# Sample attention's value products: two key heads in one stationary operand, new tokens of all sequences in two products of 512 columns

## The chip, the cores and the metric

The kernel runs on one core of a Trainium2 chip. The metric is the device time of one execution in microseconds (us). The engines are named as in the profile: PE is TensorE's matmul (PEld its weight loads), DVE VectorE, ACT ScalarE, POOL GpSimd, SP the queue of SyncE that issues most DMAs. Names such as L943 are lines of the kernel before; from L945 of it on, the changed kernel has the same code two lines earlier.

## The reference

One inference step of a hybrid decoder layer, all in float32: a prompt of 512 tokens and a sample batch of 8 sequences with 4 new tokens each pass through an input projection of 18,952 columns, an mLSTM branch (4 heads of 512), an attention branch (32 heads of 64, 4 key heads, a window of 128), and a gated merge with two projections, an output projection and a layer norm. The change lies in the attention of the sample batch:

```python
def _swa_sample(q, k_new, v_new, k_buf, v_buf, slopes, sinks):
    k_all = jnp.concatenate([k_buf, k_new], axis=1)
    v_all = jnp.concatenate([v_buf, v_new], axis=1)   # 128 kept rows and 4 new ones per sequence
    ...
    out = _sink_attend(q, k_all, v_all, dist, valid, slopes, sinks)

def _sink_attend(q, k, v, dist, valid, slopes, sinks):
    s = jnp.einsum('...qhgd,...khd->...hgqk', q, k) * (A_HEAD_DIM ** -0.5)
    ...
    p = jax.nn.softmax(jnp.concatenate([s, sink], axis=-1), axis=-1)[..., :-1]
    return jnp.einsum('...hgqk,...khd->...qhgd', p, v)
```

The last einsum is what the change computes in another way: per sequence and key head, 64 value columns, and 8 query heads times 4 tokens = 32 rows of probabilities over 128 kept and 4 new positions.

## The kernel before

The activations of all 544 tokens lie transposed in SBUF, and the columns of the input projection are worked through in pairs of 128 (function paired). A pair takes seven steps, the seven products of a Strassen-like scheme on half matrices; each step (half_product) multiplies one 128x1024 weight tile, split into a high and a low part, with 272 columns: 16 products on L634 and 8 on L636. The weights are loaded by SP (L205, L605) into a few buffers, summed by DVE (L614), cast to the high part by ACT (L212) and subtracted for the low part by DVE (L213). The results of a step are gathered on ACT, DVE and POOL (L644 to L663).

Beside this stream run Python generators: the prompt's attention, then the sample batch's (sample_attention), then the mLSTM state of the samples (samples). After each step a tick resumes every generator until its next yield; what it then emits stands in PE's program behind that step. PE's order is this order, written by hand; the other engines' order is chosen by a scheduler that goes by its own estimate of times.

In sample_attention the probabilities of the kept positions lie in E (128 rows = 32 heads x 4 tokens, per sequence 128 columns), those of the new positions in En (per sequence 32 columns, zero outside the own 4). The kept values are vb (128 positions, per sequence 4 key heads x 64), the new values of all sequences vas (32 rows). For each pair of sequences PE turns E and En (L929, L930), ACT and DVE copy the turned tiles out of PSUM (L934, L935), and two ticks later PE multiplies, per sequence and key head, vb's 64 columns with 32 columns of the turned E (L943) and adds vas's 64 columns times 32 columns of the turned En (L944). The 64 result rows of a key head go to the lower or the upper half of one PSUM tile by the tile position. So four groups of four transposes and four groups of 16 products stand between projection steps. At the end DVE multiplies the results into the gates gas (L950), SP stores them (L951), the pools t1 and t2 are closed, and the pools of the state are opened: its tiles C are loaded on SP (L990), the samples' q, k and v too (L1016), POOL makes four copies of k and v (L1000), and PE starts with L1028. Small PSUM tiles (sm) have four banks.

Of the kernel before, what the change touches and what calls it, by code (L numbers as in the profile page):

```python
# [15 lines left out]
F32 = mybir.dt.float32  # L16
# [6 lines left out]
NB = 8  # L23
# [8 lines left out]
KVH = 4  # L32
GRP = 8
# [47 lines left out]
def _build(tc, nc, i, o, es):  # L81
# [3 lines left out]
    def pool(stack, name, bufs, space=None, side=None):  # L85
        kw = {"space": space} if space is not None else {}
        if space is None:
            kw["side"] = side or "right"
            kw["reuse_waits"] = "tile"
        return stack.enter_context(tc.tile_pool(name=name, bufs=bufs, **kw))  # L90

    y_p, y_s, C_p, n_p, m_p, kb_p, vb_p, C_s, n_s, m_s, kb_s, vb_s = o
    V, A, G, PE = nc.vector, nc.scalar, nc.gpsimd, nc.tensor
# [29 lines left out]
    def nm(s):  # L123
        count[0] += 1
        return f"{s}_{count[0]}"

    def sm():
        return psB.tile([128, 512], F32, tag="sm", name=nm("sm"))
# [10 lines left out]
    def blk(ap, n=4):  # L139
        return ap.rearrange("p (b x) -> p b x", b=n)  # L140
# [21 lines left out]
    ident = cc[:, C_ID:C_ID + 128]  # L162
# [146 lines left out]
    for g in range(4):  # L309
# [9 lines left out]
        for q in range(4):  # L319
            pt = sm()  # L320
# [524 lines left out]
    esT = ExitStack()  # L845

    def sample_attention():
        t1, t2 = pool(esT, "t1", 1), pool(esT, "t2", 1)
        gas = t1.tile([128, 16, NS], F32, name="gas")
        qraw = t1.tile([128, 2, GRP, NS], F32, name="qraw")  # L850
        qas = t1.tile([128, 2, NB, GRP, NTS], F32, name="qas")
        kas = t1.tile([128, 2, NS], F32, name="kas")
        vas = t1.tile([32, 256], F32, name="vas")
        nc.sync.dma_start(gas[:], d_bra[:, :, SEQ:T].rearrange("k p t -> p k t"))
        nc.sync.dma_start(kas[:], d_ka[:, :, SEQ:T].rearrange("k p t -> p k t"))
        nc.sync.dma_start(vas[:], d_vr[SEQ:T])
        for kvh in range(KVH):
            half = slice((kvh % 2) * 64, (kvh % 2) * 64 + 64)
            for a in range(2):
                nc.sync.dma_start(qraw[half, kvh // 2, a::2],  # L860
                                  d_qa[kvh * 4:kvh * 4 + 4, a * 64:a * 64 + 64].rearrange("k p t -> p k t"))
        kb = t1.tile([128, NB, 256], F32, name="kb")
        vb = t1.tile([128, NB, 256], F32, name="vb")
        nc.sync.dma_start(kb[:], i["state_attn_k"].rearrange("b t k d -> t b (k d)"))
        nc.sync.dma_start(vb[:], i["state_attn_v"].rearrange("b t k d -> t b (k d)"))
        E = t1.tile([128, NB, 132], F32, name="E")
        En = t1.tile([128, NB, NS], F32, name="En")
        G.memset(En[:], 0.0)
        st = t1.tile([128, 4, NB], F32, name="sast")
        for _ in range(5):  # L870
            yield
        for j in range(2):
            V.tensor_scalar(qas[:, j], qraw[:, j].rearrange("p g (b t) -> p b g t", t=NTS), 0.125, None, op0=ALU.mult)

        def keysT(b2_):
            kTs = []
            for bb in range(2):
                pk = sm()
                for kk in range(2):
                    PE.transpose(pk[:, kk * 128:kk * 128 + 128], kb[:, b2_ * 2 + bb, kk * 128:kk * 128 + 128], ident)  # L880
                kT = t1.tile([128, 2, 128], F32, tag=f"kT{bb}", name=nm("kT"))
                A.copy(kT[:].rearrange("p a b -> p (a b)"), pk[:, 0:256])
                kTs.append(kT)
            return kTs

        kTs = keysT(0)
        for b2_ in range(4):
            yield
            ps_, pn_ = sm(), sm()
            for bb in range(2):  # L890
                b = b2_ * 2 + bb
                for kvh in range(KVH):
                    r = slice((kvh % 2) * 64, (kvh % 2) * 64 + 64)
                    q = qas[r, kvh // 2, b].rearrange("p g t -> p (g t)")
                    orow = slice(kvh * 32, kvh * 32 + 32)
                    tp = ((kvh % 2) * 64, kvh * 32)
                    PE.matmul(ps_[orow, bb * 128:bb * 128 + 128], q, kTs[bb][r, kvh // 2], start=True, stop=True, tile_position=tp)
                    PE.matmul(pn_[orow, bb * 4:bb * 4 + 4], q, kas[r, kvh // 2, b * 4:b * 4 + 4], start=True, stop=True, tile_position=tp)
            sl = slice(b2_ * 2, b2_ * 2 + 2)
            V.tensor_tensor(out=E[:, sl, 0:128], in0=blk(ps_[:, 0:256], 2),  # L900
                            in1=cc[:, C_SB:C_SB + 128].unsqueeze(1).to_broadcast([128, 2, 128]), op=ALU.add)
            V.tensor_tensor(out=E[:, sl, 128:132], in0=blk(pn_[:, 0:8], 2),
                            in1=cc[:, C_SB + 128:C_SB + 132].unsqueeze(1).to_broadcast([128, 2, 4]), op=ALU.add)
            if b2_ < 3:
                kTs = keysT(b2_ + 1)
        V.tensor_reduce(st[:, 0], E[:], mybir.AxisListType.X, ALU.max)
        V.tensor_scalar(st[:, 0], st[:, 0], sinkc[:], -1.0, op0=ALU.max, op1=ALU.mult)
        for b in range(NB):
            A.activation(E[:, b], E[:, b], AF.Exp, bias=st[:, 0, b:b + 1], accum_out=st[:, 1, b:b + 1])
            if b % 2:  # L910
                yield
        V.tensor_scalar(st[:, 2], st[:, 0], sinkc[:], None, op0=ALU.add)
        A.activation(st[:, 2], st[:, 2], AF.Exp)
        V.tensor_tensor(out=st[:, 1], in0=st[:, 1], in1=st[:, 2], op=ALU.add)
        V.reciprocal(st[:, 1], st[:, 1])
        for b in range(NB):
            V.tensor_scalar(En[:, b, b * 4:b * 4 + 4], E[:, b, 128:132], st[:, 1, b:b + 1], None, op0=ALU.mult)
            A.activation(E[:, b, 0:128], E[:, b, 0:128], AF.Copy, scale=st[:, 1, b:b + 1])
            if b % 2:
                yield  # L920
        for _ in range(3):
            yield
        po = sm()
        for b in range(NB):
            if b % 2 == 0:
                PTs = []
                for bb in range(2):
                    pt = sm()
                    PE.transpose(pt[:, 0:128], E[:, b + bb, 0:128], ident)  # L929
                    PE.transpose(pt[:32, 128:256], En[:, b + bb], ident)  # L930

                    p_, t_ = (t1, "kT") if b % 4 else (t2, "PT")
                    PT = p_.tile([128, 2, 128], F32, tag=f"{t_}{bb}", name=nm("PT"))[:].rearrange("p a b -> p (a b)")
                    A.copy(PT[:, 0:128], pt[:, 0:128])  # L934
                    V.tensor_copy(PT[:32, 128:256], pt[:32, 128:256])  # L935
                    PTs.append(PT)
                yield
                yield
            PT = PTs[b % 2]
            for kvh in range(KVH):  # L940
                dst = po[(kvh % 2) * 64:(kvh % 2) * 64 + 64, (kvh // 2) * 256 + b * 32:(kvh // 2) * 256 + b * 32 + 32]
                tp = (0, (kvh % 2) * 64)
                PE.matmul(dst, vb[:, b, kvh * 64:kvh * 64 + 64], PT[:, kvh * 32:kvh * 32 + 32], start=True, stop=False, tile_position=tp)  # L943
                PE.matmul(dst, vas[:, kvh * 64:kvh * 64 + 64], PT[:32, 128 + kvh * 32:160 + kvh * 32], start=False, stop=True, tile_position=tp)  # L944
        for kvh in range(KVH):  # L945
            src = po[(kvh % 2) * 64:(kvh % 2) * 64 + 64, (kvh // 2) * 256:(kvh // 2) * 256 + 256].rearrange(
                "p (b g t) -> p g b t", b=NB, g=GRP)
            for a in range(2):
                gv = gas[a * 64:a * 64 + 64, kvh * 4:kvh * 4 + 4].rearrange("p k (b t) -> p k b t", t=NTS)
                V.tensor_tensor(out=gv, in0=src[:, a::2], in1=gv, op=ALU.mult)  # L950
        nc.sync.dma_start(d_bra[:, :, SEQ:T].rearrange("k p t -> p k t"), gas[:])  # L951
# [851 lines left out]
```

## Time and profile before

| | us |
|---|---|
| median of 3 runs | 2522.78 (2520.69 to 2524.19) |
| the profiled execution | 2525.29 |
| its span | 2523.5 |
| PE busy | 2479.2 |
| DVE busy | 1779.1 |
| ACT busy | 1212.5 |
| POOL busy | 366.8 |

The span runs from the first to the last instruction of the profiled execution. Busy times are of that execution; engines work side by side, so they don't add up to the span. Matmuls are pipelined and overlap in the profile, so the distance from one start to the next, not the duration of one, tells what it costs. The chain of work that ended last is followed back from the last instruction, at each step to what released it.

### The profile page before, as it was taken

Reading aid. Unit: us, or ns where it says so; the run is one execution under the profiler, and the core shown is the slowest. Engines: PE = TensorE matmul, PEld = TensorE weight load, DVE = VectorE, ACT = ScalarE, POOL = GpSimd, SP = SyncE. Lnnn points to the kernel's source line nnn. Section 1 sums busy time; section 2 is a strip of 40 time slices with the busy share of each in tenths; the row PEclk is TensorE's granted clock in tenths of the full one; section 3 lists DMA queues with packets and bytes.
Section 4 is the critical chain, followed back from the end, with each engine's and each line's share of the span. In section 5 each row is a group of like instructions: output and inputs, shape, how many; then the busy total and the mean of one; then the engine's idle time right before and its main releaser. Section 6 shows DMA issues by size and latency. Waiting matters only on the chain.

```text
span 2523.5 us, 48930 instructions
## 1 busy us (share of the span) xinstructions
PE 2479.2 (98%) x19803; PEld 2416.3 (96%) x19803; DVE 1779.1 (71%) x2614; ACT 1212.5 (48%) x1971; POOL 366.8 (15%) x442
## 2 busy tenths in 40 slices
PE   8999999999999999999999999999999998999997
PEld 7999999999999999998999999999999998999997
DVE  7867777777677687588787888877765655776336
ACT  4447667667667665443433444344633323434221
POOL 2111111111111120131111121200000011110002
PEclk9999999999999999999999999999999999999998
DMA  6566666666666655478586775884645567988332
GB/s 192 136 167 149 162 152 154 157 152 154 158 151 154 157 123 146 105 231 249 161 260 197 223 232 146 254 246 127 190 160 165 165 206 201 254 208 240 101 98 82
DMA packets 548323, 439.20 MB, mean 174 GB/s; under 512 B 44256, under 2 KB 459280, under 8 KB 547808
## 3 DMA queue, kind: packets, MB, share of 16 engines
q1 hardware_dynamic: 535392, 389.85, 52.6%
q0 software_dynamic: 12704, 46.21, 10.0%
q8 instruction: 156, 2.56, 0.4%
q14 instruction: 71, 0.58, 0.1%
HBM read 302.68 MB, written 90.32 MB: 156 GB/s over the span
## 4 chain that ended last, share of the span: by engine, by line
PE 88%; DMA 3%; DVE 3%; issue 1%; ACT 1%; SPq 0%; POOL 0%; DVEq 0%; ACTq 0%
PE bank L634 42%; PE bank L636 21%; PE bank L229 11%; PE sm L1319 2%; PE sum L1130 1%; PE sm L1351 1%; PE sm L1364 1%; PE sm L744 1%; PE sm L784 1%; PE sm L774 1%; PE bank L1729 1%; PE sm L229 1%; DVE wl L213 1%; DMA d_n<-fr 1%; PE sm L1135 1%
## 5 line engine op out<-in xcount | busy, mean ns | idle before, releaser
L212 ACT CAST wh<-raw 128x1024 fp32r<-128x1024 f32 x628 | 657.7, 1048 | 887.5 <-PE bank L634 589.0
L213 DVE TENSOR_TENSOR wl<-raw,wh 128x1024 fp32r<-128x1024 f32 x628 | 780.4, 1244 | 296.6 <-ACT wh L212 295.1
L614 DVE TENSOR_TENSOR raw<-raw,raw 128x1024 f32<-128x1024 f32 x234 | 297.1, 1270 | 31.5 <-DMA raw<-in_w_proj_m 18.8
L634 PE MATMUL bank<-xk,wh 128*128 128x272 f32 x2304 | 315.8, 289 | 1.6 <-DVE ev L659 1.6
L634 PEld LDWEIGHTS bank<-xk,wh 128*128 128x128 f32 x2304 | 297.8, 188 | 4.5 <-ACT wh L212 1.8
L653 POOL TENSOR_TENSOR ev<-p,ev 128x272 f32<-128x272 f32 x80 | 113.7, 1422 | 564.5 <-ACT ev L652 527.6
L636 PE MATMUL bank<-xk,wl 128*128 128x272 f32 x1152 | 167.1, 287 | 0.0
L636 PEld LDWEIGHTS bank<-xk,wl 128*128 128x128 f32 x1152 | 153.5, 188 | 0.0
L634 PE MATMUL bank<-n2h,wh 128*128 128x272 f32 x576 | 147.4, 289 | 2.0 <-ACT wh L212 2.0
L634 PE MATMUL bank<-a11h,wh 128*128 128x272 f32 x576 | 148.8, 290 | 0.0
L634 PE MATMUL bank<-s4h,wh 128*128 128x272 f32 x576 | 148.6, 291 | 0.0
L634 PE MATMUL bank<-s1h,wh 128*128 128x272 f32 x576 | 148.6, 291 | 0.1
L634 PE MATMUL bank<-a11l,wh 128*128 128x272 f32 x576 | 147.8, 289 | 0.0
L634 PE MATMUL bank<-n3h,wh 128*128 128x272 f32 x576 | 147.5, 289 | 0.0
L634 PE MATMUL bank<-n3l,wh 128*128 128x272 f32 x576 | 146.9, 288 | 0.0
L634 PE MATMUL bank<-s4l,wh 128*128 128x272 f32 x576 | 146.7, 287 | 0.0
L634 PE MATMUL bank<-n2l,wh 128*128 128x272 f32 x576 | 146.6, 287 | 0.0
L634 PE MATMUL bank<-s1l,wh 128*128 128x272 f32 x576 | 146.6, 287 | 0.0
L612 POOL DMA_DIRECT2D raw<-raw x86 | 74.5, 867 | 407.6 <-DVE raw L614 173.7
L659 DVE SCALAR_TENSOR_TENSOR ev<-bank,ev 128x272 f32<-128x272 f32 x80 | 35.3, 442 | 120.1 <-PE bank L636 118.3
L229 PE MATMUL bank<-bh,wl 128*128 128x272 f32 x512 | 110.1, 292 | 7.9 <-DVE wl L213 7.9
L634 PEld LDWEIGHTS bank<-n2h,wh 128*128 128x128 f32 x576 | 108.2, 188 | 3.2 <-ACT wh L212 2.2
(503 smaller groups left out, 5953.4 us busy)
## 6 DMA issues: line engine op xcount, KB each, us to landing
raw<-in_w_in SPq DMA_DIRECT2D x296, 512.0 KB
raw<-raw POOLq DMA_DIRECT2D x86, 512.0 KB, 4.9
C<-in_state_mlstm_C SPq DMA_DIRECT2D x32, 1024.0 KB
out<-C SPq DMA_DIRECT2D x64, 512.0 KB
raw<-in_w_proj_a SPq DMA_DIRECT2D x32, 512.0 KB
raw<-in_w_proj_m SPq DMA_DIRECT2D x32, 512.0 KB
raw<-in_w_out SPq DMA_DIRECT2D x32, 512.0 KB
d_sgm<-ev SPq DMA_DIRECT2D x16, 272.0 KB
```

Of the source, the lines that this page charges most:

```text
L212: state["wh"] = A.copy(wh[:], raw[:])
L213: state["wl"] = V.tensor_tensor(out=wl[:], in0=raw[:], in1=r32(wh[:]), op=ALU.subtract)
L229: PE.matmul(ps[ALL, f, 0:w], a[:, kk], b(k, c, w), start=(k == 0 and n == 0), stop=(k == 15 and n == 2))
L612: G.dma_start(out=w[out][:], in_=w[b][:], accum_op=ALU.add)
L614: V.tensor_tensor(out=w[out][:], in0=w[a][:], in1=w[b][:], op=ALU.add)
L634: PE.matmul(ps, wh[:, k], x(p, k), start=(first and k == 0 and p == 0), stop=False, skip_group_check=True)
L636: PE.matmul(ps, wl[:, k], x(0, k), start=False, stop=(k == 7), skip_group_check=True)
L653: G.tensor_tensor(out=c22, in0=p1, in1=c11, op=ALU.subtract)
L659: V.scalar_tensor_tensor(c22, B0, -sc, c22, op0=ALU.mult, op1=ALU.add)
L744: PE.matmul(pp[:, c0 + w0:c0 + 256], qs[a][:, j * 128:j * 128 + 128], kx[:, k0:k0 + 256 - w0], start=(n == 0), stop=(n == 1))
L774: PE.transpose(pt[:, (m - m0_) * 128:(m - m0_) * 128 + 128], s_[:, b, 128:256] if own else s_[:, b + 1, 0:128], ident)
L1319: PE.matmul(pp[:, 0:258], a[:, b * 128:b * 128 + 128], b_[:, b, f], start=(b == 0 and n == 0), stop=(b == 3 and n == 2))
```

## The change

The probabilities of all sequences are turned first, En and then E, in four groups of four transposes that fill one PSUM bank each; DVE copies the first group of each, ACT the second, into one tile that reuses the buffer of the kept keys (tag kb). The pool t2 is gone. Then the new tokens of all eight sequences are multiplied at once: for two key heads together, vas's 128 columns are the stationary operand and 512 columns of the turned En the moving one, once per pair of key heads. Then follow, per pair of key heads, eight products, one per sequence: vb's 128 columns stationary, 64 columns of the turned E moving, added to the same bank. Each stationary operand holds two key heads and meets the probabilities of both; of the result the quarter blocks in which head and probabilities match are used. There are two result banks instead of one. The number of yields stays the same.

```diff
     def sample_attention():
-        t1, t2 = pool(esT, "t1", 1), pool(esT, "t2", 1)
+        t1 = pool(esT, "t1", 1)
...
-        kb = t1.tile([128, NB, 256], F32, name="kb")
+        kb = t1.tile([128, NB, 256], F32, tag="kb", name="kb")
...
-        po = sm()
-        for b in range(NB):
-            if b % 2 == 0:
-                PTs = []
-                for bb in range(2):
-                    pt = sm()
-                    PE.transpose(pt[:, 0:128], E[:, b + bb, 0:128], ident)
-                    PE.transpose(pt[:32, 128:256], En[:, b + bb], ident)
-
-                    p_, t_ = (t1, "kT") if b % 4 else (t2, "PT")
-                    PT = p_.tile([128, 2, 128], F32, tag=f"{t_}{bb}", name=nm("PT"))[:].rearrange("p a b -> p (a b)")
-                    A.copy(PT[:, 0:128], pt[:, 0:128])
-                    V.tensor_copy(PT[:32, 128:256], pt[:32, 128:256])
-                    PTs.append(PT)
+        turned = t1.tile([128, NB, 256], F32, tag="kb", name="turned")
+        PT, PN = turned[:, 0:4].rearrange("p a b -> p (a b)"), turned[:32, 4:8].rearrange("p a b -> p (a b)")
+        for src, dst, n in ((En, PN, 32), (E, PT, 128)):
+            for q in range(2):
+                pt = sm()
+                for b in range(4):
+                    PE.transpose(pt[:n, b * 128:b * 128 + 128], src[:, q * 4 + b, 0:n], ident)
+                (A.copy if q else V.tensor_copy)(dst[:, q * 512:q * 512 + 512], pt[:n])
                 yield
-                yield
-            PT = PTs[b % 2]
-            for kvh in range(KVH):
-                dst = po[(kvh % 2) * 64:(kvh % 2) * 64 + 64, (kvh // 2) * 256 + b * 32:(kvh // 2) * 256 + b * 32 + 32]
-                tp = (0, (kvh % 2) * 64)
-                PE.matmul(dst, vb[:, b, kvh * 64:kvh * 64 + 64], PT[:, kvh * 32:kvh * 32 + 32], start=True, stop=False, tile_position=tp)
-                PE.matmul(dst, vas[:, kvh * 64:kvh * 64 + 64], PT[:32, 128 + kvh * 32:160 + kvh * 32], start=False, stop=True, tile_position=tp)
+        yield
+        po = [sm(), sm()]
+        for kk in range(2):
+            PE.matmul(po[kk][:], vas[:, kk * 128:kk * 128 + 128], PN.rearrange("p (b x) -> p b x", b=NB)[:, :, kk * 64:kk * 64 + 64],
+                      start=True, stop=False, skip_group_check=True)
+        yield
+        for kk in range(2):
+            for b in range(NB):
+                PE.matmul(po[kk][:, b * 64:b * 64 + 64], vb[:, b, kk * 128:kk * 128 + 128],
+                          PT[:, b * 128 + kk * 64:b * 128 + kk * 64 + 64], start=False, stop=(b == NB - 1), skip_group_check=True)
+            yield
         for kvh in range(KVH):
-            src = po[(kvh % 2) * 64:(kvh % 2) * 64 + 64, (kvh // 2) * 256:(kvh // 2) * 256 + 256].rearrange(
-                "p (b g t) -> p g b t", b=NB, g=GRP)
+            src = po[kvh // 2][(kvh % 2) * 64:(kvh % 2) * 64 + 64].rearrange(
+                "p (b s g t) -> p s g b t", b=NB, s=2, g=GRP)[:, kvh % 2]
```

On PE, before: the end of the first group of products (of the second sequence of a pair), the transposes of the next pair, and the first product of the next step. PT is a turned tile, sm a PSUM tile, bank that of a projection step, a11h and a11l activations, wh the high part of the weights.

```order
L943 MATMUL sm_12178<-PT_12188,vb 64x32
L944 MATMUL sm_12178<-PT_12188,vas 64x32
L929 MATMUL sm_12273<-cc,E 128x128
L930 MATMUL sm_12273<-cc,En 32x128
L929 MATMUL sm_12279<-cc,E 128x128
L930 MATMUL sm_12279<-cc,En 32x128
L634 MATMUL bank_12290<-a11h_111,wh_12191 128x272
```

On PE, now: the end of the step ahead of the two wide products, these, the end of the next step, the first group of kept values, and the first product behind it (n2, xk and n3 name the activations of successive steps; wl is the low part of the weights; turned holds the turned probabilities).

```order
L636 MATMUL bank_12337<-n2h_124,wl_12262 128x272 x8
L935 MATMUL sm_12363<-turned,vas 128x512
L935 MATMUL sm_12364<-turned,vas 128x512
L634 MATMUL bank_12265<-xk_5_115,wh_12298 128x272
L636 MATMUL bank_12265<-xk_6_116,wl_12299 128x272 x4
L940 MATMUL sm_12363<-turned,vb 128x64 x8
L634 MATMUL bank_12337<-n3h_126,wh_12332 128x272
```

The transposes and the products no longer share a place; each group stands alone between two projection steps, and the last products stand ahead of the step that the last group stood behind.

On SP, before: from the store of gas to the loads of the second head's keys. C is the state, qs, ks and vs a head's samples, w the normaliser, d_g and gs gates, raw the weights.

```order
L951 DMA d_bra<-gas 128x16x32
L990 DMA C_12569<-in_state_mlstm_C 128x4x512
L1186 DMA d_g<-sz_12610 128x544
L605 DMA raw_1689_12752<-in_w_in 128x8x128
L1080 DMA gs_14222<-d_g 128x4x32
L1016 DMA qs_14475<-d_q 128x4x32
L205 DMA raw_12721<-in_w_in 128x8x128
L205 DMA raw_13018<-in_w_in 128x8x128
L1016 DMA ks_14476<-d_k 128x4x32
L605 DMA raw_1690_12754<-in_w_in 128x8x128
```

On SP, now, the same stretch:

```order
L949 DMA d_bra<-gas 128x16x32
L988 DMA C_12497<-in_state_mlstm_C 128x4x512
L1078 DMA gs_14150<-d_g 128x4x32
L1014 DMA qs_14403<-d_q 128x4x32
L605 DMA raw_1678_12680<-in_w_in 128x8x128
L1184 DMA d_g<-sz_12538 128x544
L1014 DMA ks_14404<-d_k 128x4x32
L205 DMA raw_12649<-in_w_in 128x8x128
L205 DMA raw_12946<-in_w_in 128x8x128
L605 DMA raw_1679_12682<-in_w_in 128x8x128
```

The store of gates and a weight load went behind two small loads, and the second head's ks ahead of two weight loads. On POOL the sum of L653 moved from ahead of the copies for the state to behind the first four-fold copy of ks. The rest of the orders is as before.

## The prediction

> **What bounds the kernel now.** I read the page first: how busy each engine is, and which engine carries the chain of work that ended last.
>
> ```profile
> PE 2479.2 (98%) x19803; PEld 2416.3 (96%) x19803; DVE 1779.1 (71%) x2614; ACT 1212.5 (48%) x1971; POOL 366.8 (15%) x442
> PE 88%; DMA 3%; DVE 3%; issue 1%; ACT 1%; SPq 0%; POOL 0%; DVEq 0%; ACTq 0%
> ```
>
> TensorE (PE) is busy for 98% of the span and carries 88% of the chain. Next I cut the time around sample attention's values into stretches. The columns are the length, busy us of each engine with instruction counts, TensorE's granted clock, the share of the DMA engines, and GB/s.
>
> ```profile
> core 0: us, PE busy (x) PEld busy (x) DVE busy (x) ACT busy (x) POOL busy (x), PEclk, DMA share, GB/s
> 1001.90:1047.60 45.70, 45.70 (x363) 42.26 (x362) 26.78 (x40) 14.41 (x24) 3.10 (x4) 0.96 0.23 63
> 1100.00:1150.00 50.00, 50.00 (x397) 45.06 (x397) 42.31 (x49) 19.17 (x24) 12.44 (x25) 1.00 0.83 259
> 1180.00:1200.00 20.00, 18.46 (x139) 15.98 (x138) 14.42 (x20) 6.72 (x9) 1.56 (x7) 1.00 0.80 238
> 1011.60:1015.10 3.50, 3.50 (x19) 3.20 (x19) 0.56 (x2) 1.09 (x3) 0.35 (x1) 0.51 0.57 150
> ```
>
> From 1001.90 to 1047.60 PE is never idle, DVE and ACT have half of the time free or more, and the DMA engines are nearly empty (0.23). So here a microsecond of PE work is a microsecond of span. One stretch of 3.5 us ran at a granted clock of 0.51. Then the chain itself, in order of time (start, length, what; x counts records):
>
> ```profile
> 1001.07 1.00 PE bank L636 x8
> 1002.50 2.00 PE bank L634 x16
> 1008.52 0.23 PE sm L943 x2
> 1012.43 0.41 PE sm L929
> 1013.47 2.77 PE bank L634 x16
> 1020.25 0.23 PE sm L943 x2
> 1023.91 0.26 PE sm L929
> 1024.50 2.01 PE bank L634 x16
> 1030.50 0.23 PE sm L943 x2
> 1034.17 0.26 PE sm L929
> 1034.75 2.01 PE bank L634 x16
> 1040.77 0.23 PE sm L943 x2
> 1044.43 2.21 PE bank L634 x16
> L943 PE MATMUL sm<-PT,vb 128*64 128x32 f32 x64 | 9.8, 235 | 0.0
> L944 PE MATMUL sm<-PT,vas 32*64 32x32 f32 x64 | 9.6, 230 | 0.0
> ```
>
> A step of the projection (16 products by the high part, 8 by the low part of the weights) takes 2.00 + 1.00 = 3.00 us. Between steps stand four groups of transposes (T) and four of value products (V). The code has 32 products on L943 and the profile 64 records: a product of plain f32 is two records.
>
> **What the change removes.** All of it is on PE.
> - V groups: 1020.25 to 1023.91 is 3.66 us, 1030.50 to 1034.17 is 3.67, 1040.77 to 1044.43 is 3.66; the first, 1008.52 to 1012.43, took 3.91. Sum 14.90.
> - T groups: 1002.07 (the end of the first row) to 1002.50 is 0.43 us, 1012.43 to 1013.47 is 1.04, 1023.91 to 1024.50 is 0.59, 1034.17 to 1034.75 is 0.58. Sum 2.64.
> - Behind the last V group the 16 products took 2.21 instead of 2.00 (0.21), behind the second T group 2.77 (0.77).
>
> Together 18.52 us. The slow clock's part is 0.25 (first V) + 0.45 (second T) + 0.77 = 1.47, so without it the groups cost 17.05.
>
> **What it adds.** Rows of products of the same kind, from the next stage's chain:
>
> ```profile
> 1062.64 0.81 PE sm L1028 x8
> 1064.37 2.00 PE bank L634 x16
> 1156.72 2.21 PE bank L634 x16
> 1195.05 0.97 PE sm L1084 x2
> 1196.37 1.99 PE bank L634 x16
> ```
>
> - Transposes: 16 as before, in four groups of four, each now alone between two steps. Alone, the first group took 0.43 and no surcharge came behind it: 4 x 0.43 = 1.72 us; behind products a group took 0.59, so at most 2.36.
> - New tokens: two f32 products of 512 columns. L1084 is one such product, 0.97 us: 1.94. Behind it the steps keep their length (1.99), so I add no surcharge; with one of 0.21 it is 2.15.
> - Kept values: two groups of 8 f32 products, stationary 128x128, moving 128x64. The nearest row is L1028, also f32 with a stationary 128x128 but 32 moving columns: 8 records in 0.81 us, 0.101 each. A group of 16 records is then 1.62. Twice the moving columns should hide under the weight load; if not, I bound a record by 0.125 us, a projection product with 272 columns (16 in 2.00), which makes 2.00. Behind each I put the 0.21 that the sample stage's products leave (the row of 2.21): 2 x 1.83 = 3.66, between 2 x 1.62 = 3.24 and 2 x 2.21 = 4.42.
>
> Sum 1.72 + 1.94 + 3.66 = 7.32 us, between 6.90 and 8.93.
>
> **The slow clock.** The cut stood in a stretch where PE was busy by its records, behind the first long run of small products; V2 to V4 escaped. The Trainium skill (TensorE: Matmul & The Clock Gate, section "What's actually happening") says that the clock halves when a free-running window of about 3.4 us was idle; the trace's 3.5 us at 0.51 agrees in size, but no row shows PE idle there. I take it that long runs of small products can count as idle. The longest new run is about 2.0 us against 3.9 before, so the likeliest is that the 1.47 goes too. If it comes back, the saving is 17.05 - 7.32 = 9.73 instead of 18.52 - 7.32 = 11.20.
>
> **What I cost at nothing.** Eight ACT copies and eight DVE copies of transposes become two each.
>
> ```profile
> L934 ACT COPY PT<-sm 128x128 f32<-128x128 f32 x8 | 2.0, 266 | 12.0 <-PE sm L930 12.0
> L498 ACT COPY ev<-sm 128x512 f32<-128x512 f32 x2 | 1.2, 586 | 2.7 <-PE sm L494 2.7
> L1332 DVE TENSOR_TENSOR f<-sm,cc 128x512 f32<-128x512 f32 x4 | 2.7, 682 | 0.0
> ACT wh L212 <- PE bank L634: 21.0, 10, 4.8
> DVE wl L213 <- ACT wh L212: 8.1, 4, 3.3
> ```
>
> A copy of 512 columns is about 0.6 us on ACT and, by the nearest DVE row, 0.7 on DVE. The last transposes are copied three projection steps (9 us) before the first product that reads them; without that cover PE would wait 0.6. Behind the DVE copy of a T group stands the low part of the next weights, which waits for ACT's cast and that for PE (the two rows of waits), about 2 us later; so 0.7 fits. The products of gas move earlier into two fours, each behind its value group, and their store with them. SP's queue behind that store moves along.
>
> The value products now hold two of the four small PSUM banks until gas is done, but only from the 512-column products on; the next user (L1028) comes six steps behind the last step of this section, 18 us. That the second pool is gone only shifts addresses.
>
> **The other ways.**
>
> *Weight loads by columns.* The stationary operands are twice as wide. If a load of 128 columns cost twice one of 64, a record of the new groups would take twice L943's spacing (3.66 us for 32 records, 0.114): 0.23, a group 3.66 + 0.21 and both 7.74. Added 1.72 + 1.94 + 7.74 = 11.40, saving 5.65 to 7.12: 2517.1 to 2515.7 us. Against it stands L1028: 128 columns at 0.101, closer together than 64 columns at 0.114. The Trainium skill has the rule (the same page, section "LDWEIGHTS (loading the stationary operand)"): a load takes its columns over 1.2 GHz, 53 ns for 64 and 107 for 128. By it the kept values save nothing, 64 loads of 53 against 32 of 107; these rows don't bear that out. Chance 0.07.
>
> *DMA takes it back.* Later the state streams through at 0.83 and 0.80 of the DMA engines, and PE waits there:
>
> ```profile
> 1181.44 7.00 DMA raw<-in_w_in
> 1193.78 1.27 PE L636 MATMUL bank<-a11h,wl 128*128 128x272 f32 x8 [1.54 <-DVE wl L213]
> 1046.90 0.37 SPq L951 DMA_DIRECT2D d_bra<-gas  x1
> 1047.36 0.94 SPq L990 DMA_DIRECT2D C<-in_state_mlstm_C  x1
> 1056.76 1.89 SPq L205 DMA_DIRECT2D raw<-in_w_in  x2
> 1058.35 0.61 POOL L1000 COPY rep<-ks 128x512 f32<-128x512 f32 x1
> 1058.99 0.37 SPq L1016 DMA_DIRECT2D ks<-d_k  x1
> 1075.08 1.99 PE bank L634 x16
> ```
>
> If the transfers set the pace from before this section, the whole saving returns as waits: 2522.8 us, or 1.5 either way, since the wait may also go or double. Against it: that wait is 1.54 us in all, the DMA engines stand at 0.23 in the section, and the first load of the state follows gas's store on SP, which moves with PE. Chance 0.08.
>
> *A queue that turns it round.* On SP the next head's load of ks (L1016) now stands ahead of two weight loads (L205), and it must wait for POOL's copy of the first head's ks (L1000). Before, the weight loads went at 1056.76 and ks at 1058.99, right behind that copy. The product that needs them starts at 1075.08, 18.3 us after their issue; less 7.00 for the landing (the raw load of this chain, at 0.80 of the DMA engines), 11.3 are left, from which one sum on DVE and one cast on ACT still go. PE would begin to wait beyond some 11 us of delay, and the change would end slower by 0.2% from 11 + 11.2 + 5 = 27 us on: over 2527.8 us. Against it: the copy on POOL now stands ahead of a sum (L653) that it stood behind, and ahead of it are only small copies. Chance 0.03.
>
> **How the numbers follow.** The profiled execution took 2525.29 us (span 2523.5), 2.51 above the median of the runs, 2522.78. Against its own time the sum gives 2525.29 - 11.20 = 2514.1; from the median, whose runs may or may not have had the slow stretch, 2522.78 - 11.20 = 2511.6, which I forecast (chance 0.82). If those runs were without it, or the new one gets it, it is 2513.1. The range: the largest saving by the bounds, 18.52 - 6.90 = 11.62, with the later wait of 1.54 gone, is 2509.6; the smallest, 17.05 - 8.93 = 8.12, is 2514.7, and the case of loads by columns reaches 2517.1. The runs before scatter from 2520.69 to 2524.19, so I add 1.5 below and 0.9 above: 2508 to 2518. About 0.2%, 5 us, is what a measurement of this kernel can tell from no change. Faster by more than that: 0.88 (the forecast's 0.82 and 0.06 of the loads by columns); within it 0.09 (the other 0.01 and DMA's 0.08); slower 0.03.
>
> **What would show it.** In the changed profile: no PE idle from the first T group to the state stage; two groups of kept values near 1.6 us each, the two products of 512 columns near 1.9, four T groups near 0.43, the steps between at 3.00, and a granted clock near 1.00 through the section. Value groups of 3.7 would show loads by columns; a longer wait at the weights in the state stage, DMA; SP standing before ks, the queue. A section that is shorter by 10 us in a span that isn't would make the prediction wrong.

## The result and the profile after

| | before | changed |
|---|---|---|
| median, us (5 runs each) | 2523.66 (2520.69 to 2527.73) | 2512.80 (2510.00 to 2514.19) |
| the profiled execution, us | 2525.29 | 2510.62 |
| its span, us | 2523.5 | 2508.8 |
| PE busy, us | 2479.2 | 2468.9 |

The ratio is 0.9948, with a 95% interval of 0.9933 to 0.9962: 10.9 us less by the medians. The forecast was 2511.6 us, 11.20 less, in a range of 2508 to 2518.

The chain of the changed kernel through the same place, in order of time (start, length, what; x counts records):

```profile
1000.67 0.44 PE sm L929 x4
1004.11 0.44 PE sm L929 x4
1007.54 0.44 PE sm L929 x4
1010.97 0.44 PE sm L929 x4
1011.40 2.02 PE bank L634 x16
1017.41 1.91 PE sm L935 x4
1019.32 2.21 PE bank L634 x16
1022.52 1.73 PE sm L940 x16
1024.25 2.06 PE bank L634 x16
1027.31 1.73 PE sm L940 x16
1029.04 2.05 PE bank L634 x16
1032.09 2.02 PE bank L634 x16
```

Four groups of transposes (L929), the two wide products (L935), two groups of kept values (L940), and behind each the next projection step. The section, as I call it, runs from the first transposes to the end of the eighth step behind their start or, where a group of products follows that step directly, as before, to the end of that group. Here it ends at 1032.09 and is 1032.09 - 1000.67 = 31.42 us long: eight steps of 3.00 and 7.42 us of its own. Before, it ran from 1002.07 to 1044.43, 42.36 us, of which 1.47 were the slow clock's, so 40.89 without. The difference of 10.94 us, with the 0.21 that lay behind the last group of before, is 11.15.

The same stretch by windows (length, busy us of PE, PEld, DVE, ACT, POOL, PEclk, DMA share, GB/s), and the later one in which PE had waited 1.54 us for weights:

```profile
1000.60:1017.40 16.80, 16.80 (x138) 16.55 (x136) 14.21 (x15) 8.33 (x12) 3.13 (x4) 1.00 0.26 78
1017.40:1020.80 3.40, 3.40 (x17) 2.15 (x17) 1.62 (x3) 0.10 (x1) 0.00 (x0) 1.00 0.62 166
1020.80:1032.10 11.30, 11.30 (x96) 11.30 (x96) 6.95 (x13) 3.46 (x4) 0.00 (x0) 1.00 0.34 91
1170.00:1190.00 20.00, 20.00 (x154) 17.88 (x153) 17.57 (x24) 7.58 (x10) 2.95 (x7) 1.00 0.71 214
```

PE is never idle in them and the granted clock is 1.00. On SP and POOL, the next head's ks and the weight loads behind it, from the timelines:

```profile
1031.38 0.37 SPq L949 DMA_DIRECT2D d_bra<-gas  x1
1040.66 0.61 POOL L998 COPY rep<-ks 128x512 f32<-128x512 f32 x1
1041.30 0.36 SPq L1014 DMA_DIRECT2D ks<-d_k  x1
1044.41 1.81 SPq L205 DMA_DIRECT2D raw<-in_w_in  x2
```

The store of gas goes out 15.5 us earlier than the 1046.90 of before, and ks right behind POOL's copy. No wait of PE follows.

The two profiled spans differ by 14.7 us, 3.8 more than the medians. Of that, 1.40 lies ahead of the section (it begins at 1000.67 instead of 1002.07; in a second profile of the kernel before, e1 below, at 1000.16), 11.15 in it, 1.54 is the wait that was gone in this execution, and 0.6 lies elsewhere. Such a wait comes again in e2, e3 and e5 below (1.8 us each), in e9 (1.6) and, with 0.6 us, in e11, which is the changed kernel itself. So I don't count it as the change's.

### The profile page after: what moved, and what is told of

Same layout as the page of the kernel before. It is cut to its first block, busy times and chain, and to the rows that moved or that the text cites. A ratio compares the mean times of both kernels' runs of the same rounds, so it can differ in the third digit from the quotient of the medians.

```text
span 2508.8 us, 48732 instructions
## 1 busy us (share of the span) xinstructions
PE 2468.9 (98%) x19711; PEld 2408.4 (96%) x19711; DVE 1778.4 (71%) x2608; ACT 1211.9 (48%) x1965; POOL 366.5 (15%) x442
## 4 chain that ended last, share of the span: by engine, by line
PE 89%; DMA 3%; DVE 2%; issue 1%; ACT 1%; SPq 0%; POOL 0%; DVEq 0%; ACTq 0%; POOLq 0%
PE bank L634 43%; PE bank L636 21%; PE bank L229 11%; PE sm L1317 2%; PE sum L1128 1%; PE sm L1349 1%; PE sm L1362 1%; PE sm L744 1%; PE sm L784 1%; PE bank L1727 1%; PE sm L774 1%; PE sm L229 1%; DMA d_n<-fr 1%; PE sm L1133 1%; DVE wl L213 1%
## 5 line engine op out<-in xcount | busy, mean ns | idle before, releaser
L653 POOL TENSOR_TENSOR ev<-p,ev 128x272 f32<-128x272 f32 x80 | 115.1, 1439 | 564.0 <-ACT ev L652 530.2
```

The source lines that it names most:

```text
L653: G.tensor_tensor(out=c22, in0=p1, in1=c11, op=ALU.subtract)
```

## The experiments

The theory that I took into them was that a small f32 product costs its two records at about 0.11 us each, whatever its columns, so that fewer products are the gain. The rival: weight loads go by stationary columns, and something else made the old groups slow. A second question was whether long runs of small products lower the clock. e1 to e7 and e10 were executed once each (2530.42, 2515.85, 2512.13, 2511.94, 2528.79, 2512.01, 2520.60 and 2510.97 us), so I compare their sections: single times are too coarse for 1 us, as e2 and e3 show, where the shorter section has the longer time.

**e1: the kernel before, profiled a second time.** No edit.

> The kernel before, unchanged, profiled a second time. From the first transposes of the values (L929) to the start of the step behind the last group of value products its section took 42.36 us in the first profile, 1.47 of them by a stretch at half clock that began in the first group. Theory (long runs of small products count as idle time for the clock, in a window that runs free): such a stretch comes again, but in any of the four groups, or, if no window fits, not at all: 42.4 or 40.9 us. Rival (something at that place in the program causes it): it begins again within the first group, 42.4 us. Rival (an accident): none in the section, 40.9 us.

Its section ran from 1000.16 to 1048.33: 48.17 us. From the chain, its start, the start of the first group, the first products at the lower clock, and the step behind the last group; then windows of the trace:

```profile
1000.16 0.11 PE sm L929
1006.61 0.23 PE sm L943 x2
1008.90 0.33 PE sm L943 x2
1048.33 2.21 PE bank L634 x16
```

```profile
1003.00:1009.00 6.00, 6.00 (x51) 5.45 (x50) 5.97 (x8) 2.39 (x3) 0.00 (x0) 0.99 0.00 0
1009.00:1012.40 3.40, 3.40 (x19) 2.89 (x19) 0.73 (x3) 0.60 (x3) 0.00 (x0) 0.50 0.54 144
1012.40:1015.80 3.40, 3.40 (x17) 3.40 (x16) 0.24 (x1) 0.54 (x2) 1.35 (x1) 0.51 0.12 42
1022.60:1029.40 6.80, 6.80 (x33) 6.42 (x33) 0.74 (x3) 1.41 (x3) 0.00 (x0) 0.50 0.28 77
1036.30:1039.70 3.40, 3.40 (x18) 3.18 (x17) 0.56 (x2) 0.53 (x2) 0.00 (x0) 0.51 0.41 121
```

The clock was halved three times, in or behind the first three groups, for 6.8, 6.8 and 3.4 us; all its borders lie on one grid of 3.4 us. That cost 48.17 - 40.89 = 7.3 us, against 1.47 in the first profile. So the cuts come again, neither at one place nor by a single accident, and their size changes from run to run. PE was busy by its records in all of these stretches.

**e2: kept values by key head again.** In the changed kernel:

```diff
-                PE.matmul(po[kk][:, b * 64:b * 64 + 64], vb[:, b, kk * 128:kk * 128 + 128],
-                          PT[:, b * 128 + kk * 64:b * 128 + kk * 64 + 64], ...)
+                for h in range(2):
+                    PE.matmul(po[kk][h * 64:h * 64 + 64, b * 64 + h * 32:b * 64 + h * 32 + 32],
+                              vb[:, b, kk * 128 + h * 64:kk * 128 + h * 64 + 64],
+                              PT[:, b * 128 + kk * 64 + h * 32:b * 128 + kk * 64 + h * 32 + 32], ..., tile_position=(0, h * 64))
```

> The changed kernel, but the kept values by single key heads again: 32 f32 products of 64 stationary and 32 moving columns in place of 16 of 128 and 64. The section took 31.42 us in the changed kernel, the two groups 1.73 each. Theory (a small product costs its two records at about 0.11 us each, whatever its columns): 32 records a group, 3.65 us each, section 31.42 + 3.8 = 35.3 us, and 1.5 more if a group meets the clock's window. Rival (a product costs its weight load, and that goes by stationary columns): 32 loads at half the price, 1.7 us a group, section 31.4 us.

```profile
1001.30 0.44 PE sm L929 x4
1023.15 1.05 PE sm L941 x32
1024.20 2.21 PE bank L634 x16
1027.41 1.06 PE sm L941 x32
1028.46 2.20 PE bank L634 x16
1031.67 2.01 PE bank L634 x16
```

A group of twice the products took 1.05 us instead of 1.73, 0.033 a record; behind it lie 0.2 instead of 0.06. Section 1001.30 to 1031.67: 30.37 us, 1.05 less than the changed kernel. My theory falls: products of half the columns cost less than half. The rival's 1.7 us a group was missed as well; e10 shows why. Putting two key heads into one operand made the kept values dearer, not cheaper.

**e3: new tokens by sequence and key head again.** In the changed kernel:

```diff
-            PE.matmul(po[kk][:], vas[:, kk * 128:kk * 128 + 128], PN...[:, :, kk * 64:kk * 64 + 64], start=True, ...)
+            for b in range(NB):
+                for h in range(2):
+                    PE.matmul(po[kk][h * 64:h * 64 + 64, b * 64 + h * 32:b * 64 + h * 32 + 32],
+                              vas[:, kk * 128 + h * 64:kk * 128 + h * 64 + 64],
+                              PN[:, b * 128 + kk * 64 + h * 32:b * 128 + kk * 64 + h * 32 + 32], start=(b == 0), ..., tile_position=(0, h * 64))
```

> The changed kernel, but the new tokens by sequence and key head again: 32 f32 products of 64 stationary and 32 moving columns in one group in place of two of 512 moving columns (1.91 us and 0.21 behind them). Theory (records): 64 records, 7.3 us, section 31.42 + 5.2 = 36.6 us; a run of 7.3 us always holds a whole window of the clock, so about 1.7 us more and a granted clock near 0.5 for some 3.4 us: 38.3 us. Rival (loads by columns): 64 loads at 0.053, 3.4 us, section 32.7 us. Rival on the clock (an accident): 1.00 throughout, 36.6 us.

```profile
1019.27 1.98 PE sm L937 x64
1021.26 2.21 PE bank L634 x16
```

32 small products took 1.98 us, the two wide ones 1.91; section 1002.53 to 1034.03, 31.50 us. So the wide products save 0.07, and the theory (7.3 us for the run) falls a second time; the rival's 3.4 us wasn't met either. 64 records of products with 32 rows cost 0.031 each, so such products aren't dear by themselves. The run was too short to say anything on the clock.

**e4: by key head, and all in one run.** As e2, without the yields between the wide products and the two groups (they follow behind).

> The changed kernel with the kept values by single key heads, and all value products in one place, behind the two wide products, with no projection step between: 32 small products, 64 records, in one run. Theory (records; small products count as idle for the clock): 7.3 us for the run, at least one whole window within it at a granted clock near 0.5, section 31.42 + 3.8 + 1.7 = 36.9 us or more. Rival on the clock (an accident): 1.00, 35.2 us. Rival (loads by columns): 3.5 us for the run, section 31.3 us.

```profile
1019.03 1.91 PE sm L935 x4
1020.93 1.99 PE sm L940 x64
1022.92 2.20 PE bank L634 x16
```

1.99 us for the 64 records, where the theory had 7.3 and the rival 3.5; section 1002.29 to 1032.11, 29.82 us: 0.55 less than e2, mostly the surcharges behind separate groups. The clock stayed at 1.00; the run of small products was again too short for a window.

So single products of the old shape are cheap when they stand among their like. What the old groups had besides was the alternation: kept values (128 rows), then new tokens (32 rows), into the same place. Three kernels take that apart. All use the changed kernel's transposes and two banks; their groups are

```python
        for g in range(4):
            items = [(b, kvh) for b in (g * 2, g * 2 + 1) for kvh in range(KVH)]
            for n, item in enumerate(items):
                part(*item, True)                          # kept: vb, 128 rows
                part(*items[(n + shift) % 8], False)       # new: vas
            yield
```

**e5: alternating as before** (shift 0).

> The changed kernel's transposes and result banks, but the value products as before: per sequence and key head one product with the kept values (128 rows, 64 stationary and 32 moving columns) and right behind it one with the new tokens (32 rows) into the same place; four groups of 16, a projection step between. Groups of such products by key head without alternation took 1.05 us (16 of them, kept values) and 1.98 (32, new tokens). Theory (the alternation costs: of row counts or of writing the same place twice in a row): 3.66 us a group, as before, at full clock. Rival (something else of the old code, one bank for all or its start and stop marks, cost it): about 1.05 us a group.

```profile
1033.89 3.67 PE sm L937 x32
1040.76 3.67 PE sm L937 x32
```

The two groups at full clock took 3.67 us, as in the kernel before. The first two (4.00 and 3.81 us) fell into cuts of the clock.

**e6: alternating, all with 128 rows** (shift 0; vas and the turned En padded with zeros to 128 rows).

> As e5_alternating, but the new tokens' operands are padded with zeros to 128 rows, so that all products have 128 rows; they still write the same place in pairs. Theory (row counts): the alternation is gone, about 1.05 us a group. Rival (the same place twice in a row): 3.66 us a group as in e5.

```profile
1014.54 1.08 PE sm L939 x32
1027.36 1.07 PE sm L939 x32
```

These are the first and the last group; the two between took 1.08 us each.

**e7: alternating rows, never the same place twice in a row** (shift 4: the same key head of the other sequence).

> As e5_alternating (rows 128 and 32 by turns, the same half of the array), but the product behind each kept one belongs to the same key head of the other sequence of the pair, so that no two neighbours write the same place. Theory (row counts): still 3.66 us a group. Rival (the same place twice in a row): about 1.05 us a group.

```profile
1014.63 3.67 PE sm L937 x32
1035.22 3.67 PE sm L937 x32
```

The two groups between took 3.67 us as well.

e6 and e7 together decide it. With equal row counts the pairs into the same place cost 1.08 us a group; with 128 and 32 rows by turns they cost 3.67, even into different places. It is the change of row counts from product to product: 0.115 us a record instead of 0.034. What the engine does at such a change no row shows.

**e9: the kernel before, rows alone.** Nothing of the change, only zeros:

```diff
-        vas = t1.tile([32, 256], F32, name="vas")
+        vas = t1.tile([128, 256], F32, name="vas")
+        G.memset(vas[:], 0.0)
...
-        nc.sync.dma_start(vas[:], d_vr[SEQ:T])
+        nc.sync.dma_start(vas[:32], d_vr[SEQ:T])
...
+                    G.memset(PT[:, 128:256], 0.0)
...
-                PE.matmul(dst, vas[:, ...], PT[:32, 128 + kvh * 32:160 + kvh * 32], start=False, stop=True, tile_position=tp)
+                PE.matmul(dst, vas[:, ...], PT[:, 128 + kvh * 32:160 + kvh * 32], start=False, stop=True, tile_position=tp)
```

> The kernel before with one difference: the new tokens' values and turned probabilities are padded with zeros to 128 rows, so that the products no longer alternate between 128 and 32 rows. Everything else, the order, the 128 small products, the copies, is as before. Theory (row counts by turns are what the old groups paid for): four groups of 1.08 us instead of 3.66, section 40.89 (at full clock) less 10.3 = 30.6 us, 0.8 under the changed kernel; no clock below 1.00 in it; time 0.994 to 0.995 of before, as the changed kernel. Rival (two key heads in one operand and the two wide products are needed for the gain): no more than the clock's part, 0.997 to 1.000.

Ratio 0.9942 (0.9926 to 0.9957), median 2510.71 us. From the chain, the first transposes, then the beginning of the second group and the row behind it, and the same of the last:

```profile
1000.30 0.11 PE sm L930
1014.41 0.24 PE sm L945 x4
1014.66 0.12 PE sm L946 x4
1015.49 0.26 PE sm L930
1029.75 0.24 PE sm L945 x4
1030.82 2.21 PE bank L634 x16
```

1014.41 to 1015.49 and 1029.75 to 1030.82, 1.08 and 1.07 us. Section 1000.30 to 1030.82: 30.52 us, as forecast (30.6), at a granted clock of 1.00, and 0.90 less than the changed kernel's, or 0.69 with the surcharge behind its last group. The 64 small products in the old order (128 are their records, not the products as the expectation has it) do with zeros all that the change does.

**e10: the halves in a row.** As e2, but with the loop over h outside that over b: eight products in one half of the array, then eight in the other.

> As e2_kept_by_head, but a group takes its eight products of one half of the array first and then the eight of the other, instead of the halves by turns (1.05 us a group, 0.033 a record). Theory (the two halves overlap, a load of 64 columns by itself costs 0.053): 32 records of about 0.053, 1.7 us a group, section 31.7 us. Rival (no overlap, 64 columns simply cost 0.033): 1.05 us a group, section 30.4 us.

```profile
1022.43 1.77 PE sm L941 x32
1027.41 1.77 PE sm L941 x32
```

0.055 us a record instead of 0.033. So 64 columns by themselves cost half of the 0.108 of 128 columns (1.73 us for 16 records). Those had 64 moving columns and these 32, but L1028, with 128 stationary and 32 moving columns, had 0.101. By turns a record costs less than it does alone in its half, which I read as an overlap of the two halves.

**e8, e11, e12: a version from these, and the changed kernel beside it.** The new tokens' probabilities are turned without their zeros and spread by DVE; their products go by key head over 256 columns, and the kept values by key head in the same run:

```diff
+        PE.transpose(pt[:32, 0:128], En[:], ident)        # En: 128 x 32, no zeros
+        V.tensor_tensor(out=PN..., in0=pt[:32, 0:128]..., in1=cc[0:32, C_M8:C_M8 + NB]..., op=ALU.mult)
...
+        for kvh in range(KVH):
+            PE.matmul(quarter_of(kvh), vas[:, kvh * 64:kvh * 64 + 64], PN...[:, :, kvh * 32:kvh * 32 + 32],
+                      start=True, ..., tile_position=(0, (kvh % 2) * 64))
+        for kk in range(2):
+            for b in range(NB):
+                for kvh in (kk * 2, kk * 2 + 1):
+                    PE.matmul(quarter_of(kvh)[:, b], vb[:, b, kvh * 64:kvh * 64 + 64], PT[...], ...)
```

> A version put together from the runs so far: the new tokens' probabilities are turned once, without their zeros, and spread by DVE with a mask (one transpose for eight); the new tokens by key head in four products of 64 stationary and 256 moving columns; the kept values by key head, 32 products, in the same run. Theory (products by key head in the two halves of the array overlap): transposes 0.11 + 0.87, new tokens 0.9, kept values 2.0, 0.2 behind them: section 28.0 us against 31.42 of the changed kernel, the whole about 3.4 us less, 0.993 to 0.994 of before. Rival (the wide products of two halves don't overlap): new tokens 1.8, section 28.9 us.

> The changed kernel again, beside the next one on the same chip: section 31.4 us, clock 1.00 in it, 0.9948 of before within the earlier interval. If the clock's cuts in the kernel before make up part of the gain, its own runs scatter less than those of before.

> The version of e8 again, beside the changed kernel on the same chip: section 28.2 us against 31.4, so some 3.2 us (0.13%) under e11. Rival (the 5.7 us between the two medians of different calls is the version's own): 5 us or more under e11.

The chain of e12:

```profile
1002.36 0.11 PE sm L925
1008.50 0.44 PE sm L933 x4
1018.37 1.01 PE sm L943 x8
1019.38 1.99 PE sm L949 x64
1021.37 2.20 PE bank L634 x16
1030.55 2.02 PE bank L634 x16
```

The section ends at 1030.55 and takes 28.19 us (28.20 in e8), as expected; that of the changed kernel in e11 31.42 again. The four products of 256 columns took 1.01 us, not the 1.8 expected without an overlap, so the halves overlap there too.

| on one chip | median, us | runs, us | ratio to before |
|---|---|---|---|
| before (11 runs) | 2525.76 | 2521.51 to 2533.18 | |
| e11, changed | 2511.84 | 2510.96 to 2514.03 | 0.9946 (0.9930 to 0.9962) |
| e9, rows alone | 2510.71 | 2509.04 to 2515.88 | 0.9942 (0.9926 to 0.9957) |
| e12, put together | 2507.08 | 2505.50 to 2508.65 | 0.9924 (0.9908 to 0.9940) |

e12 is the fastest; e8 had 0.9922 (0.9908 to 0.9936). Its runs lie below all of e11's. By the medians it is 4.8 us under the changed kernel, by the section 3.2; the other 1.6 lie within the scatter of the runs (about 3 us in both), and where they come from wasn't tried. The runs of before spread over 11.7 us, as they would if the clock's cuts made part of the gain; but those of e9, whose section has no cut in its profile, spread over 6.8.

## Why the prediction was right, point by point

- **PE decides here.** Right: the section's gain of 11.15 us is found again in the medians (10.9), and no wait took it back. That the two lie so close is partly luck, as the point on the clock shows. One reading was off: DVE was busy for 26.78 of 45.70 us, 59%, so it hadn't half of the time free; it didn't matter, since PE never waited for it in the section.
- **What goes.** Read off the trace, right: 18.52 us with the slow clock.
- **What comes.** Forecast 7.32, measured 7.42. Transposes 1.72 against 1.73 (four groups of 0.43 to 0.44). The two wide products 1.94 against 1.91, but with 0.21 behind them that I had given them only as a bound. The kept values 2 x 1.62 against 2 x 1.73, and 0.06 and 0.05 behind them where I had put 0.21: 3.66 against 3.57. The kept values' nearest row (0.101 a record) was too low by 0.007.
- **The clock.** The cut went, as I took to be likeliest. Its size was wrong: I read 1.47 us from one profile, and the second shows 7.3. Part of the gain is thus not a number of the kernel's but varies with the runs of before. At full clock the section gained 40.89 + 0.21 - 31.42 = 9.68 us; the medians show 1.2 us more in the first comparison and 4.2 in the last. The clock explains only part of the 4.2: the granted clock over a whole run has a median of 0.992 for the eleven runs of before and of 0.9935 for the six of e11. That is, as an estimate, 3.8 us less at half clock, and at e1's rate (7.3 us lost in 17.0 at half clock) 1.6 us of time. The rest stays open.
- **The rival of loads by columns.** Here the prediction failed, though its number held. It set L1028 (128 columns, 0.101) against L943 (64 columns, 0.114) and concluded that spacing doesn't go by columns. But L943's 0.114 was no price of a load: e6 and e7 show that the turns of row counts set it. Free of them a record costs 0.055 at 64 columns in one half (e10), 0.033 in two halves by turns (e2), and 0.108 at 128. So the rule that I weighed and set aside holds where one half is loaded at a time: the Trainium skill (TensorE: Matmul & The Clock Gate, section "LDWEIGHTS (loading the stationary operand)") gives 53 and 107 ns, and these runs agree. The rival's price was wrong as well, since it doubled the wrong row. The 7.32 us held because the rows behind its terms stand apart from such turns, and because what goes was read off the trace, whatever made it slow. What the rule says of the kept values holds too: as wide products they save nothing (1.73 us a group against 1.77 in e10).
- **What the change is.** I costed it as what its words say, fewer and wider products. e9 shows that neither the two heads in one operand nor the wide products carry the gain: equal row counts in the old order bring 0.9942. The change gains because it puts all products of 32 rows apart from those of 128; the two heads in one operand cost 1.05 us of it back (e2), and the wide products are worth 0.07 (e3).
- **DMA, and SP's queue.** Neither came about: the state's first load moved with gas's store (1031.84 us instead of 1047.36), and ks went right behind POOL's copy.

## What to carry to other kernels

Price a group of instructions by a row of the same neighbourhood: the spacing of small products tells what stands next to them as much as what they are. On TensorE, keep products of one row count together, or pad with zeros to the larger count, and send those that fill half of the columns to the two halves by turns. A second profile of the kernel before would have shown that a slow stretch read from one execution is a sample and no constant.

## What the hardware showed that I had not expected

- **Row counts by turns.** f32 products of 128 and 32 rows in alternation cost 0.115 us a record, the same with 128 rows all through 0.034 (e5, e7 against e6, e9).
- **Halves of the columns overlap.** 0.033 us a record by turns against 0.055 in a row (e2, e10). In e6 and e9 two products in a row went to the same half, and a record still cost 0.034. The Trainium skill (the same page, section "The mechanism") lets weight loads overlap with running products only where the row groups differ. By that sentence alone the halves, which have the same rows here, wouldn't overlap; these runs say they do. Whether a load overlaps with the other half's load or with its product isn't told apart.
- **The clock falls while PE is busy by its records.** In e1 it was halved at 1008.9, behind a stretch of 3.4 us (from 1005.5 on its grid) of which the small alternating products filled 2.3, from 1006.61 on. In the first profile the stretch from 1032.1 to 1035.5 (the same grid from its cut at 1011.7) held 2.0 us of them and 0.6 of transposes, and passed. In e7 no cut came: its groups start 6.87 us apart, two stretches of the grid, and by the cuts elsewhere in its trace each group was split into about 2.1 and 1.6 us. So the threshold lies, as an estimate from these traces, between 2.1 and 2.3 us of 3.4, and transposes don't count as these products do. Whether it is the small share of the array, the 32 moving columns or the turns of row counts that counts as idle is open: no run without the turns was long enough.
